# Rolling an 8192 x 8192 array: three of sixteen row groups taken through SBUF instead of copied inside HBM

## The chip, the cores and the metric

One core of one Trainium2 chip runs the program. Times are device microseconds (us) of that core; the number for a kernel is the median over its runs. "HBM" is the large memory in which the input and the output lie, "SBUF" the core's own memory of 128 partitions. "DMA" is a transfer: an instruction on one of the core's queues that 16 DMA engines of the core then carry out. Three queues issue such instructions here: SP (SyncE), ACT (ScalarE) and POOL (GpSimd). No TensorE work is done.

## The reference

```python
def setup_inputs():
    return {"x": np.random.randn(8192, 8192).astype(np.float32), "shift": 100}

def reference(x, shift):
    return np.roll(x, shift, axis=1)
```

Each row of 8192 float32 numbers (32,768 bytes) is rotated right by 100 columns: columns 100 to 8191 of the output are columns 0 to 8091 of the input, and columns 0 to 99 are the last 100 of the input. Nothing is computed; 268.44 MB are read and 268.44 MB are written.

## The kernel before

With the shift `s` = 100, `a` = 128 is the shift rounded up to a multiple of 128, and `g` = `a - s` = 28. Each output row is made in two parts: the **body**, columns 128 to 8191 (32,256 bytes), and the **head**, columns 0 to 127 (512 bytes).

**The body** is copied from HBM to HBM without passing through SBUF (L36 to L41). The rows stand in 128 blocks of 64 rows. One DMA takes the 16 rows `c*64 + e*4 + j` for e = 0 to 15, one row for each DMA engine, 504 KB in all; j runs over 0 to 3, and even j go to the SP queue, odd j to the ACT queue (L41). In the last four blocks each row is cut in two at column `mid`, so these DMAs are of 248 and 256 KB (L38). That is 528 DMAs, 264 on each queue. They depend on nothing but a free place: the framework hands eight completion semaphores round to the DMAs of SP and ACT together, and a DMA whose semaphore is still in use waits on its queue until the earlier DMA with it has landed. So at most eight of these DMAs are under way, four to a queue.

**The heads** go through SBUF on the POOL queue (L58 to L78), in 16 groups of 512 rows, four rows to a partition. For each group, POOL issues a load of 512-byte pieces that holds the tail of one row and the start of the next (`t`, L70), a load of the last row's 100 columns (L71) and a load of the first row's 28 columns (L74); VectorE (DVE) puts the pieces together in `h` (L72, L75). After the loads of all 16 groups, POOL issues 16 stores of 256 KB (L78).

Of the kernel before, what the change touches and what calls it, by code (L numbers as in the profile page):

```python
# [1 line left out]

# [4 lines left out]


@with_exitstack
def kernel(  # L10
    ctx: ExitStack,
    tc: tile.TileContext,
    x: bass.AP,
    shift: int,
    out: bass.AP,
):
    nc = tc.nc
    n_rows, n_cols = x.shape
    s = shift % n_cols
    a = -(-s // 128) * 128  # L20
    g = a - s
    P = nc.NUM_PARTITIONS
    engines = [nc.sync, nc.scalar]
    n_chunks = 16
    rows = n_rows // n_chunks

    xm = x.rearrange("(c e j) w -> c j e w", e=16, j=4)
    om = out.rearrange("(c e j) w -> c j e w", e=16, j=4)
    if a < n_cols:
        blocks = n_rows // 64
        mid = (a + n_cols) // 256 * 128  # L36
        for c in range(blocks):
            parts = ((a, mid), (mid, n_cols)) if c >= blocks - 4 and a < mid else ((a, n_cols),)  # L38
            for j in range(4):
                for lo, hi in parts:  # L40
                    engines[j % 2].dma_start(out=om[c, j, :, lo:hi], in_=xm[c, j, :, lo - s:hi - s])  # L41
    if a == 0:
        return


    if a > 512:
        for i in range(n_chunks):
            r = slice(i * rows, (i + 1) * rows)
            nc.gpsimd.dma_start(out=out[r, :s], in_=x[r, n_cols - s:])
            if g > 0:  # L50
                nc.gpsimd.dma_start(out=out[r, s:a], in_=x[r, :g])
        return

    Q = 4  # L58
    n_st = n_rows // (P * Q)
    reads = ctx.enter_context(tc.tile_pool(name="reads", bufs=n_st))  # L60
    heads = ctx.enter_context(tc.tile_pool(name="heads", bufs=n_st))
    xt = x.rearrange("(k p q) c -> k p q c", q=Q, p=P)
    ot = out.rearrange("(k p q) c -> k p q c", q=Q, p=P)
    tiles = []
    for k in range(n_st):
        t = reads.tile([P, Q - 1, a], x.dtype)
        h = heads.tile([P, Q, a], x.dtype)
        lead = bass.AP(tensor=x.tensor, offset=(k * P * Q + 1) * n_cols - s,
                       ap=[[Q * n_cols, P], [n_cols, Q - 1], [1, a]])
        nc.gpsimd.dma_start(out=t[:], in_=lead, single_packet=True)  # L70
        nc.gpsimd.dma_start(out=h[:, Q - 1, :s], in_=xt[k, :, Q - 1, n_cols - s:], single_packet=True)  # L71
        nc.vector.tensor_copy(h[:, :Q - 1, :s], t[:, :, :s])  # L72
        if g > 0:
            nc.gpsimd.dma_start(out=h[:, 0, s:], in_=xt[k, :, 0, :g], single_packet=True)  # L74
            nc.vector.tensor_copy(h[:, 1:, s:], t[:, :, s:])  # L75
        tiles.append(h)
    for k, h in enumerate(tiles):
        nc.gpsimd.dma_start(out=ot[k, :, :, :a], in_=h[:], single_packet=True)  # L78


# [1 line left out]
_INS = ['x', 'shift']  # L82
_OUTS = [((8192, 8192), 'float32')]

_NUMBERS = {'shift': 100}


# [26 lines left out]
```

## Time and profile before

| | |
|---|---|
| Median of 3 runs | 830.12 us (828.03 to 830.18) |
| Profiled execution: span from first to last instruction | 818.3 us |
| Profiled execution: time outside that span | not printed; the median lies 11.8 us above the span |
| DVE busy | 7.8 us, 32 instructions |
| POOL busy | 41.1 us, 68 instructions |
| DMAs of the body, issue to landing | 12.5 us (median, 504 KB) |
| Loads of `t` on POOL, issue to landing | 32.6 us (median, 192 KB) |
| Stores of `h` on POOL, issue to landing | 63.0 us (median, 256 KB) |
| Issuing one DMA: SP, ACT | 510 ns, 517 ns (median) |

How to read it: the line "DMA" of the page gives, in 40 equal slices, the busy share of the 16 DMA engines in tenths, and "GB/s" what they moved. The part on queues gives for each queue its packets, its bytes and the time that its packets took, as a share of the time of all 16 engines: q1 and q10 are the queues of SP and ACT (the body), q0 that of POOL (the heads). A DMA from HBM to HBM counts once in the bytes that the engines moved, and twice in the traffic of HBM, for it is read there and written there. The same answers can be had for any stretch of the span, and rates below are made from them: bytes of a stretch by its length, or bytes of a queue by the engine time that its share stands for (share times 16 engines times length).

### The profile page before, as it was taken

Reading aid. Unit: us, or ns where it says so; the run is one execution under the profiler, and the core shown is the slowest. Engines: PE = TensorE matmul, PEld = TensorE weight load, DVE = VectorE, ACT = ScalarE, POOL = GpSimd, SP = SyncE. Lnnn points to the kernel's source line nnn. Section 1 sums busy time; section 2 is a strip of 40 time slices with the busy share of each in tenths; the row PEclk is TensorE's granted clock in tenths of the full one; section 3 lists DMA queues with packets and bytes.
Section 4 is the critical chain, followed back from the end, with each engine's and each line's share of the span. In section 5 each row is a group of like instructions: output and inputs, shape, how many; then the busy total and the mean of one; then the engine's idle time right before and its main releaser. Section 6 shows DMA issues by size and latency. Waiting matters only on the chain. (4 is left out here: it accounts for less than half of the span.)

```text
span 818.3 us, 689 instructions
## 1 busy us (share of the span) xinstructions
DVE 7.8 (1%) x32; POOL 41.1 (5%) x68
## 2 busy tenths in 40 slices
DVE  0000000000000000000000000000000000000000
POOL 3011111111010000000000000000000000000000
DMA  9999999999999999999999999999999999999998
GB/s 304 340 344 338 341 334 345 341 346 350 353 352 357 347 332 321 335 328 326 333 330 323 330 331 330 331 326 333 330 328 334 333 330 339 328 333 334 328 318 294
DMA packets 20229, 272.71 MB, mean 333 GB/s; under 512 B 9472, under 2 KB 9728, under 8 KB 11776
## 3 DMA queue, kind: packets, MB, share of 16 engines
q1 hardware_dynamic: 8448, 132.14, 48.2%
q10 hardware_dynamic: 8448, 132.14, 46.1%
q0 software_dynamic: 3328, 8.39, 4.7%
q14 instruction: 5, 0.04, 0.0%
HBM read 268.44 MB, written 268.44 MB: 656 GB/s over the span
## 5 line engine op out<-in xcount | busy, mean ns | idle before, releaser
L78 POOL DMA_DIRECT2D out_dram<-h x16 | 11.4, 712 | 87.2 <-DMA out_dram<-h 51.7
L70 POOL DMA_DIRECT2D t<-in_x_dram x16 | 12.1, 759 | 32.1 <-DMA h<-in_x_dram 31.3
L74 POOL DMA_DIRECT2D h<-in_x_dram x16 | 8.6, 538 | 85.7 <-DMA t<-in_x_dram 85.7
L71 POOL DMA_DIRECT2D h<-in_x_dram x16 | 8.9, 558 | 23.9 <-DMA h<-in_x_dram 23.9
L72 DVE COPY h<-t 128x300 f32<-128x300 f32 x16 | 5.9, 368 | 190.4 <-DMA t<-in_x_dram 190.4
L75 DVE COPY h<-t 128x84 f32<-128x84 f32 x16 | 3.2, 201 | 0.0
L95 POOL MEMSET const-float32-0.0<- 128x1 f32 x1 | 0.1, 99 | 0.2 <-issue 0.2
L95 POOL MEMSET const-bfloat16-1.0<- 128x1 bf16 x1 | 0.1, 101 | 0.0
L95 POOL MEMSET const-uint8-127<- 128x1 uint8 x1 | 0.1, 99 | 0.0
L95 POOL MEMSET const-float32-1.0<- 128x1 f32 x1 | 0.1, 98 | 0.0
## 6 DMA issues: line engine op xcount, KB each, us to landing
out_dram<-in_x_dram ACTq DMA_DIRECT2D x248, 504.0 KB, 12.5
out_dram<-in_x_dram SPq DMA_DIRECT2D x248, 504.0 KB, 12.5
out_dram<-h POOLq DMA_DIRECT2D x16, 256.0 KB, 63.0
t<-in_x_dram POOLq DMA_DIRECT2D x16, 192.0 KB, 32.6
out_dram<-in_x_dram SPq DMA_DIRECT2D x8, 256.0 KB, 5.9
out_dram<-in_x_dram ACTq DMA_DIRECT2D x8, 256.0 KB, 5.8
out_dram<-in_x_dram SPq DMA_DIRECT2D x8, 248.0 KB, 6.1
out_dram<-in_x_dram ACTq DMA_DIRECT2D x8, 248.0 KB, 6.1
```

The lines of the kernel that those rows point to most:

```text
L70: nc.gpsimd.dma_start(out=t[:], in_=lead, single_packet=True)
L71: nc.gpsimd.dma_start(out=h[:, Q - 1, :s], in_=xt[k, :, Q - 1, n_cols - s:], single_packet=True)
L72: nc.vector.tensor_copy(h[:, :Q - 1, :s], t[:, :, :s])
L74: nc.gpsimd.dma_start(out=h[:, 0, s:], in_=xt[k, :, 0, :g], single_packet=True)
L75: nc.vector.tensor_copy(h[:, 1:, s:], t[:, :, s:])
L78: nc.gpsimd.dma_start(out=ot[k, :, :, :a], in_=h[:], single_packet=True)
L95: nc = _bacc.Bacc("TRN2", target_bir_lowering=False, num_devices=1)
```

## The change

The last three groups of 512 rows (rows 6656 to 8191) are taken out of the copies and of the heads. Each goes whole through one SBUF tile `stage` of 128 partitions by 4 rows by 8192 columns (128 KB in each partition, one buffer). A group is loaded by 17 DMAs: the last 100 columns of all its rows (`wrap`, pieces of 400 bytes), then 16 pieces of 128 partitions by 2048 columns (`load`, 1 MB each, rows of 8192 bytes in a partition), already shifted by 100 columns in SBUF; the last of each row has 1948 columns. It is stored by 16 DMAs of 128 by 2048 (`store`). Loads and stores are issued by SP and ACT, in one sequence with the copies, which alternates between the two queues.

The order is written out in advance: six phases, load and store of each of the three groups, each with one sixth of the copies; after each move so many copies are issued as are due. A store waits for the loads whose columns it holds, and a load of the next group for the stores that read its place. The 416 blocks-and-j of copies that remain cover rows 0 to 6655; the last two blocks, not the last four, have their rows cut at `mid`. The heads of 13 groups stay on POOL as they were (L96 to L104 of the changed file).

```diff
-    engines = [nc.sync, nc.scalar]
+    rings = [nc.sync, nc.scalar]
+    n_staged = 3
+    n_copied = n_groups - n_staged
...
-        blocks = n_rows // 64
-        for c in range(blocks):
-            parts = ((a, mid), (mid, n_cols)) if c >= blocks - 4 and a < mid else ((a, n_cols),)
-            for j in range(4):
-                for lo, hi in parts:
-                    engines[j % 2].dma_start(out=om[c, j, :, lo:hi], in_=xm[c, j, :, lo - s:hi - s])
+    def copy(c, j, lo, hi):
+        return lambda ring: ring.dma_start(out=om[c, j, :, lo:hi], in_=xm[c, j, :, lo - s:hi - s])
+    blocks = n_copied * G // 64
...
+        parts = ((a, mid), (mid, n_cols)) if c >= blocks - 2 else ((a, n_cols),)
+        for j in range(4):
+            copies += [(copy(c, j, lo, hi), hi - lo) for lo, hi in parts]
+    stage = ctx.enter_context(tc.tile_pool(name="stage", bufs=1)).tile([P, Q, n_cols], x.dtype)
+    W = 2048
+    def load(k, q, lo):
+        hi = min(lo + W, n_cols - s)
+        return lambda ring: ring.dma_start(out=stage[:, q, lo + s:hi + s], in_=xt[k, :, q, lo:hi])
+    def wrap(k):
+        return lambda ring: ring.dma_start(out=stage[:, :, :s], in_=xt[k, :, :, n_cols - s:])
+    def store(k, q, lo):
+        return lambda ring: ring.dma_start(out=ot[k, :, q, lo:lo + W], in_=stage[:, q, lo:lo + W])
+    phases = []
+    for k in range(n_copied, n_groups):
+        spots = [(q, lo) for q in range(Q) for lo in range(0, n_cols, W)]
+        phases.append([wrap(k)] + [load(k, *at) for at in spots])
+        phases.append([store(k, *at) for at in spots])
+    total = sum(w for _, w in copies)
+    issued, done, todo = 0, 0, list(copies)
+    for n, side in enumerate(phases):
+        begin, end = total * n / len(phases), total * (n + 1) / len(phases)
+        for i, move in enumerate(side):
+            move(rings[issued % 2])
+            issued += 1
+            upto = begin + (end - begin) * (i + 1) / len(side)
+            while todo and done < upto:
+                one, w = todo.pop(0)
+                one(rings[issued % 2])
+                issued += 1
+                done += w
...
-    for k in range(n_st):
+    for k in range(n_copied):
```

More of the change, by code (lines that the diff above doesn't have):

```diff
@@ L22 @@
     P = nc.NUM_PARTITIONS
-    engines = [nc.sync, nc.scalar]
-    n_chunks = 16
-    rows = n_rows // n_chunks
+    rings = [nc.sync, nc.scalar]
+    Q = 4
+    G = P * Q
+    n_groups = n_rows // G
+    if a == 0 or a > 512:
+        for i in range(n_groups):
+            r = slice(i * G, (i + 1) * G)
+            rings[i % 2].dma_start(out=out[r, s:], in_=x[r, :n_cols - s])
+            if s > 0:
+                nc.gpsimd.dma_start(out=out[r, :s], in_=x[r, n_cols - s:])
+        return
+    n_staged = 3
@@ L32 @@
+    n_copied = n_groups - n_staged
+    xt = x.rearrange("(k p q) c -> k p q c", q=Q, p=P)
+    ot = out.rearrange("(k p q) c -> k p q c", q=Q, p=P)
     xm = x.rearrange("(c e j) w -> c j e w", e=16, j=4)
     om = out.rearrange("(c e j) w -> c j e w", e=16, j=4)
-    if a < n_cols:
-        blocks = n_rows // 64
-        mid = (a + n_cols) // 256 * 128
-        for c in range(blocks):
-            parts = ((a, mid), (mid, n_cols)) if c >= blocks - 4 and a < mid else ((a, n_cols),)
-            for j in range(4):
-                for lo, hi in parts:
-                    engines[j % 2].dma_start(out=om[c, j, :, lo:hi], in_=xm[c, j, :, lo - s:hi - s])
@@ L42 @@
[L42 to L62, printed above, removed]
@@ L63 @@
-    ot = out.rearrange("(k p q) c -> k p q c", q=Q, p=P)
+    def copy(c, j, lo, hi):
+        return lambda ring: ring.dma_start(out=om[c, j, :, lo:hi], in_=xm[c, j, :, lo - s:hi - s])
+    blocks = n_copied * G // 64
+    mid = (a + n_cols) // 256 * 128
+    copies = []
+    for c in range(blocks):
+        parts = ((a, mid), (mid, n_cols)) if c >= blocks - 2 else ((a, n_cols),)
+        for j in range(4):
+            copies += [(copy(c, j, lo, hi), hi - lo) for lo, hi in parts]
+    stage = ctx.enter_context(tc.tile_pool(name="stage", bufs=1)).tile([P, Q, n_cols], x.dtype)
@@ L64 @@
+    reads = ctx.enter_context(tc.tile_pool(name="reads", bufs=n_copied))
+    heads = ctx.enter_context(tc.tile_pool(name="heads", bufs=n_copied))
     tiles = []
-    for k in range(n_st):
+    for k in range(n_copied):
         t = reads.tile([P, Q - 1, a], x.dtype)
         h = heads.tile([P, Q, a], x.dtype)
-        lead = bass.AP(tensor=x.tensor, offset=(k * P * Q + 1) * n_cols - s,
+        lead = bass.AP(tensor=x.tensor, offset=(k * G + 1) * n_cols - s,
                        ap=[[Q * n_cols, P], [n_cols, Q - 1], [1, a]])
```

## The prediction, made before the changed kernel had run

> **What bounds the kernel now.** I read the page's DMA part first, then the engines, then the queues stretch by stretch. The compute engines are idle (DVE 7.8 us, POOL 41.1 us of 818.3). From the page:
>
> ```profile
> span 818.3 us, 689 instructions
> ...
> DMA  9999999999999999999999999999999999999998
> GB/s 304 340 344 338 341 334 345 341 346 350 353 352 357 347 332 321 335 328 326 333 330 323 330 331 330 331 326 333 330 328 334 333 330 339 328 333 334 328 318 294
> DMA packets 20229, 272.71 MB, mean 333 GB/s; under 512 B 9472, under 2 KB 9728, under 8 KB 11776
> ...
> HBM read 268.44 MB, written 268.44 MB: 656 GB/s over the span
> ```
>
> The DMA engines are busy in every slice. But the GB/s line has two levels: about 345 in slices 1 to 13, while the heads pass through SBUF, and 330 after. If the engines themselves were the limit, the small pieces of the heads should have lowered the rate. So I ask for the queues in three stretches: heads being loaded (20 to 174 us), heads being stored (205 to 270) and copies alone (330 to 800).
>
> ```profile
> DMA packets 4846, 52.57 MB, mean 341 GB/s; under 512 B 2190, under 2 KB 2412, under 8 KB 3333
> ...
> q1 hardware_dynamic: 1515, 24.65, 44.0%
> q10 hardware_dynamic: 1498, 24.16, 40.1%
> q0 software_dynamic: 1833, 3.76, 15.2%
> ```
> ```profile
> DMA packets 2030, 23.15 MB, mean 356 GB/s; under 512 B 790, under 2 KB 790, under 8 KB 1386
> ...
> q1 hardware_dynamic: 644, 10.42, 47.3%
> q10 hardware_dynamic: 639, 10.26, 43.0%
> q0 software_dynamic: 744, 2.44, 10.8%
> ```
> ```profile
> DMA packets 9801, 155.07 MB, mean 330 GB/s; under 512 B 4902, under 2 KB 4902, under 8 KB 4902
> ...
> q1 hardware_dynamic: 4901, 77.44, 50.4%
> q10 hardware_dynamic: 4897, 77.62, 48.9%
> ```
>
> Two numbers come out of each. First, HBM traffic, copies (q1, q10) counted twice and heads once: loading (2 x 48.81 + 3.76) / 154 = 658 GB/s; storing (2 x 20.68 + 2.44) / 65 = 674; copies alone 2 x 155.06 / 470 = 660. Within 2% it is the same. Second, what one engine moves for a copy while it works on one (bytes by share times 16 engines times length): alone 155.06 MB / (0.993 x 16 x 470) = 20.8 GB/s; beside loads 48.81 / (0.841 x 16 x 154) = 23.6; beside stores 20.68 / (0.903 x 16 x 65) = 22.0. A copy goes faster on its engine when other engines do something that loads HBM less. Both say the same: the present bound is HBM's traffic, near 660 GB/s, and the engines are "busy" with copies that wait for it.
>
> The issuing queues are no bound. SP's waits:
>
> ```profile
> SPq L41 <- DMA out_dram<-in_x_dram: 671.1, 260, 4.8
> ```
>
> 260 of its 264 DMAs wait for a place; issuing costs 264 x 0.51 = 135 us beside 671 us of waiting.
>
> **The change part by part.**
>
> *HBM traffic: nothing.* Copies: 6656 rows x 32,256 B = 214.70 MB, counted twice 429.4; heads of 6656 rows 3.41 MB in and out, 6.8; staged rows 1536 x 32,768 B = 50.33 MB in and 50.33 out, 100.7. Sum 536.9 MB, as before (2 x 268.44). At the whole-span rate of 656 GB/s: 818 us. This is the bound if only traffic decides.
>
> *Engine work: much more.* Bytes through the engines were 272.7 MB and become 214.7 + 6.8 + 100.7 = 322.2 MB. To end in 818 us the engines must move 394 GB/s; the best stretch above had 356. The room is the time in which copies now wait. How much there is, the trace bounds by the fastest copy rate of one queue: q10 beside loads, 24.16 MB / (0.401 x 16 x 154) = 24.5 GB/s for each engine, 391 for 16. At that rate for all large transfers: (214.7 + 100.7) / 391 = 807 us, plus the heads: q0 has 4.7% of the engines' time, 38.5 us, of which 13/16, 31.2. Together 838 us, and 2 us for the three `wrap` loads, whose 400-byte pieces are like the loads of the heads (0.61 MB at 3.76 / (0.152 x 16 x 154) = 10.0 GB/s for each engine: 3.8 us of all 16, against 1.6 already counted). Divided by the 99% that the engines are busy: 848 us.
>
> *Price of a staged byte.* Not shown as such: pieces of 8 KB on the hardware queues. Nearest rows: q0's stores, 2.44 / (0.108 x 16 x 65) = 21.7 GB/s for each engine with pieces of 512 B; q0's loads at 10.0; copies with pieces of 32 KB at 24.5. With 21.7 for all staged bytes, and copies at 23.6 beside loads and 22.0 beside stores: 107.35/23.6 + 107.35/22.0 + 100.7/21.7 ms over 16 engines = 879, plus 31, 910 us. That is the upper end; 10.0 belongs to 112- to 512-byte pieces and is not taken. The larger piece is nearer to the copies' 24.5.
>
> The Trainium skill, DMA: Bandwidth & Descriptors, section Specifications, gives the 16 engines a fabric ceiling of 435 GB/s; by it the large transfers would take an estimated 725 us and the engines would never bind. No row here reaches it: the highest, of one queue, is 391 for 16 engines, so the trace neither shows nor excludes it.
>
> *The sum.* HBM alone gives 818, engines at their fastest seen 848, and the two limits now lie close. A limit in such a system is not sharp: when at some moment most engines hold loads, HBM is under-used; when most hold copies, engines wait. I take the middle, span 834, 16 us more. The median of the runs shown is 11.8 us above the span (the page prints no other time for the profiled execution); I keep this. **Forecast: 846 us.**
>
> *Waits added.* Loads and stores stand in the same SP and ACT queues as the copies, so a waiting store holds the copies behind it. But a store needs loads of its columns, some 88 DMAs earlier in the joint sequence, with eight under way and 12.5 us to landing; the changed program's order gives the stores a single semaphore, and only one `wrap` has two. I take nothing. If each of the five borders emptied the queues once: 5 x 12.5 = 62 us, 880 in all.
>
> *Issuing.* 523 DMAs on SP and ACT in place of 528, hidden by the waits above. *POOL and DVE* lose 3/16: not on the path, which is DMA throughout. *Ends.* The first 20 us ran at 304 GB/s, the last 18 at 292; cuts in two blocks instead of four, and a 1 MB store among the last DMAs: 0 to 3 us, within the range.
>
> **The rivals.**
>
> *Traffic alone decides* (engines have room to spare): span 818, time 827 to 838. For it: 658, 674 and 660 stay level while q0's share of bytes goes from 0 to 10.5%. Against: from now on it would be 31%.
>
> *Faster: uneven traffic suits HBM.* Beside stores the traffic was 674, 2% over copies alone, at 10.5% of the bytes; beside loads 658, no gain. If only these levels hold: 268.4/658 + 268.4/674 = 806, with 5 us for the slow ends 811, time 823. If the gain of the stores grows with their share, threefold, to 700: 408 + 383 + 5 = 796, time 808. It decides if the engines then move over 394 GB/s. Against: this is above all that the trace shows, and loads, half of the staging, showed none of it.
>
> *One direction is capped.* A load phase reads 16.78 + 35.78 + 0.57 = 53.1 MB and writes less; the highest read rate of a stretch is 341 GB/s and the highest write rate 356. Were these caps: 3 x 53.1/341 + 3 x 53.1/356 = 915 us, time 927. For it: nothing exceeds them. Against: they are above copies alone (330), so they rose as soon as something else let them. The Trainium skill (same page, section Where 436 GB/s comes from) lets a core's share of HBM, about 358 GB/s, bind transfers between HBM and SBUF, by which the six phases would take an estimated 890 us; the 356 here lies just under it. But its HBM Reference, section Specifications (TRN2), has a core that streams alone at about 425.
>
> *It does not do what it says* (loads and copies fall apart in time): this is the case of the borders, 880 us, 892 with the rest.
>
> **How the numbers follow.** Forecast case, two soft limits, 838 to 875: 0.46. Traffic alone, 827 to 838: 0.17, of which 0.09 within 0.3% of 830.1 (2.5 us, about what a measurement of this kernel can tell from no change), 0.06 above and 0.02 below. Faster by uneven traffic, 800 to 827: 0.25. Capped direction or emptied queues, 875 to 927: 0.12. So faster 0.27, same 0.09, slower 0.64. Range 806 to 895: it leaves out the edge of the gain and most of the caps.
>
> **What would show it.** Right: phases of about 139 us, HBM traffic 640 to 655 GB/s through the span, payload near 385, copies at 24 GB/s or more for each engine, engines busy over 97%. Traffic alone: 656 to 662 over the span. Faster: store phases above 674. Capped: load and store phases at 341 to 360 of one-way traffic, copies slower on their engine than 22. Borders: slices of the DMA line below 9 at each sixth. I am wrong in size if staged pieces of 8 KB take much more or less than 24.5 GB/s for each engine, and in sign if HBM gives above 665 GB/s to an uneven mix.

## The result, and the profile after

| | Before | After |
|---|---|---|
| Median | 830.15 us (828.03 to 831.99, 4 runs) | 854.43 us (852.77 to 856.33, 4 runs) |
| Ratio, 95% interval | | 1.0297 (1.0272 to 1.0322) |
| Profiled execution: time, span | not printed, 818.3 | 852.77, 851.0 |

The kernel became 3% slower. (Ratios here and below leave out an execution more than 1.5% above the fastest of its kernel; there was one, in e5_even16.) From the page of the changed kernel:

```profile
span 851.0 us, 664 instructions
...
GB/s 328 406 387 392 403 399 402 386 398 383 387 375 350 361 384 378 396 378 373 398 382 357 353 404 394 385 379 367 383 398 367 400 384 378 349 389 393 376 372 272
DMA packets 31685, 322.25 MB, mean 379 GB/s; under 512 B 10736, under 2 KB 10944, under 8 KB 14144
...
q10 hardware_dynamic: 13952, 158.87, 48.8%
q1 hardware_dynamic: 15024, 156.52, 47.9%
q0 software_dynamic: 2704, 6.82, 2.5%
...
HBM read 268.44 MB, written 268.44 MB: 631 GB/s over the span
```

The engines move 322.25 MB, as worked out, and they move them faster (379 GB/s in place of 333). HBM carries the same bytes as before, but only 631 GB/s of them in place of 656. The shares of the queues add up to 99.2%, so the engines were busy all the same. The GB/s line is more uneven than that of before: 349 beside 389, 353 beside 404. That unevenness is what the experiments are about.

### The profile page after: what moved, and what is told of

Same layout as the page of the kernel before. It is cut to its first block, busy times and chain, and to the rows that moved or that the text cites. A ratio compares the mean times of both kernels' runs of the same rounds, so it can differ in the third digit from the quotient of the medians.

```text
span 851.0 us, 664 instructions
## 1 busy us (share of the span) xinstructions
DVE 6.3 (1%) x26; POOL 33.4 (4%) x56
## 2 busy tenths in 40 slices
DMA packets 31685, 322.25 MB, mean 379 GB/s; under 512 B 10736, under 2 KB 10944, under 8 KB 14144
## 5 line engine op out<-in xcount | busy, mean ns | idle before, releaser
L104 POOL DMA_DIRECT2D out_dram<-h x13 | 9.2, 711 | 39.0 <-DMA out_dram<-h 25.0
L96 POOL DMA_DIRECT2D t<-in_x_dram x13 | 9.9, 762 | 16.3 <-DMA h<-in_x_dram 15.5
L100 POOL DMA_DIRECT2D h<-in_x_dram x13 | 7.0, 539 | 40.8 <-DMA t<-in_x_dram 40.8
L97 POOL DMA_DIRECT2D h<-in_x_dram x13 | 7.3, 558 | 9.6 <-DMA h<-in_x_dram 9.2
```

## The experiments

Three theories stood at the start. **A**: HBM traffic and the engines now limit by turns. At times most engines hold staged packets, which load HBM once, and the engines' own rate decides; at times nearly all hold copies, and HBM decides. What matters is how evenly the two are mixed. **B**: each staged byte costs engine time, however it is mixed. **C**: the loss is at the two ends of the span.

All ratios are against the kernel before, run beside the changed form on the same chip.

| Run | What differs from the changed kernel | Median, us | Before | Ratio, 95% interval |
|---|---|---|---|---|
| e0_before | (the kernel before) | 827.7 | 826.8 | one execution |
| e1_split_queues | staged moves on ACT, copies on SP, 16 KB pieces | 908.7 | 826.8 | 1.099 (1.098 to 1.101) |
| e2_w4096 | 16 KB pieces, 2 MB per DMA | 847.4 | 826.8 | 1.025 (1.022 to 1.028) |
| e3_one_group | one group | 836.8 | 826.8 | 1.013 (1.011 to 1.016) |
| e5_even16 | 16 partitions, 512 KB per DMA | 884.2 | 827.3 | 1.066 (1.058 to 1.073) |
| e5_even32 | 32 partitions, 512 KB per DMA | 834.6 | 827.3 | 1.009 (1.006 to 1.013) |
| e5_even16_one | 16 partitions, 512 KB, one group | 829.5 | 827.3 | 1.003 (1.001 to 1.004) |
| e6_fours | four staged moves at a time | 890.5 | 827.3 | 1.077 (1.074 to 1.079) |
| e7_even64 | 64 partitions, 512 KB per DMA | 826.6 | 818.7 | 1.009 (1.007 to 1.011) |
| e7_w1024 | 128 partitions, 4 KB pieces, 512 KB | 828.3 | 818.7 | 1.012 (1.010 to 1.014) |
| e8_even32_one | 32 partitions, 512 KB, one group | 818.1 | 818.7 | 1.000 (0.999 to 1.001) |
| e9_w8192 | whole rows, 4 MB per DMA | 866.3 | 828.1 | 1.047 (1.044 to 1.050) |

**The kernel before once more.**

> The kernel before, unchanged, profiled once more. The changed kernel's profiled execution took 852.8 us with a span of 851.0, so 1.8 us lie outside the span. If that is general, this execution's time is about 2 us above its span too, and the 818.3 us of the first profile belonged to an execution about 10 us below the median; then the span here is 818 to 830 us. If the kernel before really has 11.8 us outside its span, the span is near 818 and the time near 830.

```profile
span 826.0 us, 689 instructions
...
HBM read 268.44 MB, written 268.44 MB: 650 GB/s over the span
```

This execution took 827.74 us, 1.7 above its span. So the 11.8 us of the prediction were hardly time outside the span: the first profile most likely belonged to an execution some 10 us faster than the median beside it. Medians of the kernel before differ likewise between the four chips used here, 818.7 to 828.1, which is why ratios on one chip are compared below.

**Staged moves on one queue, copies on the other.**

```diff
-    W = 2048
+    W = 4096
...
-            move(rings[issued % 2])
-            issued += 1
+            move(nc.scalar)
...
-                one(rings[issued % 2])
-                issued += 1
+                one(nc.sync)
```

> Staged moves all on ACT in pieces of 16 KB (W = 4096), copies all on SP with 32 KB: an engine that takes one packet from each queue in turn always holds one staged packet to one copy, 1 to 2 in bytes, about the 31% that is to be moved. Theory A (loss from an uneven mix: both limits are close, and at times most engines hold staged packets, at times most hold copies): HBM traffic rises from 631 to 648 GB/s or more, time 820 to 838 us. Theory B (engine work: each byte that passes the engines twice costs engine time, however it is mixed): 850 to 860 us, HBM traffic near 631.

It took 908.7 us, which neither theory expected, and it did not make the mix that it was meant to make. SP's waits show why:

```profile
SPq L45 <- DMA out_dram<-in_x_dram: 394.6, 374, 1.9
SPq L45 <- DMA out_dram<-stage: 151.1, 13, 25.9
SPq L45 <- DMA stage<-in_x_dram: 128.7, 12, 12.7
```

Copies on SP waited 280 us, in 25 waits, for staged DMAs to land, since both still share the eight semaphores. The staged moves ran ahead nearly alone, until about 290 us, and the copies followed alone. So it does not tell A from B, but it measures each kind of traffic apart. Here are stretches of its trace with stores (145 to 185 us), with loads (205 to 225) and with copies only (300 to 880):

```profile
DMA packets 1151, 17.10 MB, mean 427 GB/s; under 512 B 164, under 2 KB 164, under 8 KB 164
...
q10 hardware_dynamic: 1037, 15.03, 88.5%
q1 hardware_dynamic: 114, 2.06, 12.0%
```
```profile
DMA packets 649, 8.48 MB, mean 424 GB/s; under 512 B 159, under 2 KB 159, under 8 KB 159
...
q10 hardware_dynamic: 585, 7.45, 87.5%
q1 hardware_dynamic: 64, 1.03, 12.0%
```
```profile
DMA packets 11771, 190.07 MB, mean 328 GB/s; under 512 B 5877, under 2 KB 5877, under 8 KB 5877
...
q1 hardware_dynamic: 11768, 190.04, 99.9%
```

With hardly anything but staged packets the engines move 424 to 427 GB/s in either direction; a staged packet has 26.5 GB/s of its engine (15.03 MB / (0.885 x 16 x 40 us)). That is the highest rate of the stretches read here, the engines' limit as far as the runs show, and HBM then carries (15.03 + 2 x 2.06) / 40 = 479 GB/s. Copies alone move 328, with HBM at 656. The same lines answer a rival, that a copy is simply slower on its engine than a staged packet. The few copies beside the staged packets have 2.06 / (0.120 x 16 x 40) = 26.8 GB/s of their engine, as much as these; copies alone have 190.04 / (0.999 x 16 x 580) = 20.5. So what slows a copy here is other copies, which load HBM as well. At the moments of either kind one of the two limits lies idle.

**Four staged moves at a time.** This is the plain test of A: the same DMAs on the same queues, only less evenly spread.

```diff
-            upto = begin + (end - begin) * (i + 1) / len(side)
+            upto = begin + (end - begin) * ((i + 1) // 4 * 4 if i + 1 < len(side) else len(side)) / len(side)
```

> The change with the same DMAs, but issued four staged moves at a time, two on each queue, and then the copies that are due for four: the same bytes and pieces, less evenly mixed. Theory A: more time with only staged packets and more with only copies, HBM traffic lower, 868 to 900 us (staging wholly apart from the copies took 908.7). Theory B: 850 to 860, no change.

890.5 us: A. The two kinds of stretch can be seen directly; the columns are the stretch, its length, DVE, POOL, clock, share of DMA and GB/s:

```profile
408.00:416.00 8.00, 0.00 (x0) 0.00 (x0) 1.00 1.01 409
424.00:440.00 16.00, 0.00 (x0) 0.00 (x0) 1.00 1.00 329
451.00:456.00 5.00, 0.00 (x0) 0.00 (x0) 1.00 1.00 421
464.00:480.00 16.00, 0.00 (x0) 0.00 (x0) 1.00 0.99 329
```

The timeline has four loads issued from 399 to 407 us and four stores from 443 to 451. After each burst the engines move 409 to 421 GB/s, nearly all of it staged (from 408 to 416 us the trace has 3.27 MB in 397 packets over 512 bytes, 8.2 KB each); in between they move 329, all of it copies (from 424 to 440 us 5.26 MB in 163 such packets, 32 KB each). If the whole kernel consisted of such stretches, it would take 100.7 MB / 415 + 214.7 MB / 329 = 243 + 653 = 896 us, the heads left out: this run is nearly that. Theory B, under which the same bytes take the same time, falls. The trace's records of single packets say where the time went. In the changed kernel the staged packets (7792 and 8192 bytes) took 252 us of all 16 engines and the copies' whole rows (32,256 bytes) 552; here it is 245 and 598. The staged bytes cost no more than in the changed kernel; the copies, crowded together, do.

**Smaller staged DMAs, spread more finely.** Loads and stores take every eighth, fourth or second partition (D = 8, 4, 2), or all with shorter pieces, so that each staged DMA has 512 KB, like a copy. Edit for 32 partitions:

```diff
-    W = 2048
+    W = 4096
+    D = 4
...
-        return lambda ring: ring.dma_start(out=stage[:, q, lo + s:hi + s], in_=xt[k, :, q, lo:hi])
+        return lambda ring: ring.dma_start(out=stage[b::D, q, lo + s:hi + s], in_=xt[k, b::D, q, lo:hi])
...
-        spots = [(q, lo) for q in range(Q) for lo in range(0, n_cols, W)]
+        spots = [(q, lo, b) for q in range(Q) for lo in range(0, n_cols, W) for b in range(D)]
```

With 32 partitions:

> As the run with 16 partitions, but 32 partitions (every fourth) with half rows of 16 KB: two packets for each engine, 512 KB for each staged DMA. Theory A: between that run and the change, 825 to 845 us. Theory B: 850 to 860. It also shows whether the reach of 16 partitions costs anything: then this one is the faster of the two.

834.6 us, inside A's range and outside B's: a ratio of 1.009 in place of 1.030, with the same bytes through the engines. From its page:

```profile
GB/s 338 395 401 393 398 407 399 417 404 374 384 384 405 368 380 392 384 399 389 390 398 395 385 396 391 386 379 372 383 396 393 387 386 395 380 395 390 389 392 320
...
HBM read 268.44 MB, written 268.44 MB: 646 GB/s over the span
```

The GB/s line is flatter again, near 390, and HBM is back at 646, beside 650 in e0_before. So 390 GB/s through the engines and HBM near its limit are possible together. Against the changed kernel the copies' whole rows took 534 us of all 16 engines in place of 552, which is most of the 20 us by which the span is shorter; the staged packets took 258. What the 7 us are that remain, no run takes apart.

With 16 partitions (D = 8, W = 8192):

> The staged bytes as in the change, but each staged DMA takes 16 partitions (every eighth) with whole rows of 32 KB: one packet for each engine, the same shape as a copy, and 192 such DMAs are spread among the copies, about one to two. So no engine ever has eight staged packets in a row in one queue, as it has with 128 partitions. Theory A (the loss is the uneven mix): HBM traffic 645 GB/s or more, time 822 to 840 us. Theory B (engine work of the staged bytes, however mixed): 850 to 860. If 16 partitions at a time are slower to reach than 128: over 860, with staged packets far above the 1.2 us that 32 KB need at the engines' best rate.

884.2 us: A's number missed, by the third reading that the expectation names. The trace shows which packets are slow. From its page (span 887.6 us, the longest of its four executions):

```profile
GB/s 302 329 376 340 354 333 359 379 392 395 385 369 378 383 344 383 380 333 346 352 364 380 393 389 388 378 361 327 368 336 348 357 348 369 371 374 384 381 389 304
```

The line is near 350 on average in the stretches with loads (numbers 2 to 7, 15 to 20 and 28 to 33) and near 380 in those with stores. A packet of a load (32,368 bytes) took 1.85 us on average, one of a store (32,768 bytes) 1.30. The size of the piece is not the reason: in e9_w8192, with packets of the same sizes over 128 partitions, they took 1.25 and 1.22. With 32 partitions a load packet of half the size took 0.67 us, or 1.35 for the same bytes; 0.5 us more for each of 1536 load packets is 48 us of all 16 engines, and the span is 56 us longer than there. So it is the loads into every eighth partition that are slow. Why is open. The Trainium skill, SBUF — State Buffer, section Door 1: The DMA port swizzle, ties a transfer's rate to how many of 16 SBUF ports its partitions reach; by its formula every eighth partition reaches 8 ports, every fourth all 16. The loads agree with that, but the stores, from the same partitions, show next to nothing of it, so the ports are not shown to be the cause.

With 64 partitions (D = 2, W = 2048) and with all 128 and 4 KB pieces (D = 1, W = 1024):

> As the even form with 32 partitions (834.6 us), but 64 partitions (every second) with pieces of 8 KB, the change's own piece: four packets of 8 KB for each engine, 512 KB for each staged DMA, twice as many staged DMAs as the change. Theory A (length of the run of staged packets that one DMA puts into an engine's queue decides): four against eight of the same size, 836 to 848 us, between 834.6 and 854.4. If the size of the piece decides, 850 to 856.

> All 128 partitions with pieces of 4 KB: eight packets for each engine as in the change, but half the bytes, 512 KB for each staged DMA. If the bytes of a run decide: near the other 512 KB forms, 834 to 842 us. If the number of packets in a run decides, as when engines take one packet from each queue in turn: with eight copies between eight small packets the mix is poorer still, 848 to 865.

1.009 and 1.012. (In us these expectations assumed a kernel before at 827; here it took 818.7. As ratios to 827 the 836 to 848 and 834 to 842 expected of 512 KB are 1.011 to 1.025 and 1.008 to 1.018: the first result lies just under its range, the second inside.) Neither the size of a packet nor the number of packets in a run decides: four packets of 8 KB are as good as two of 16, and eight of 4 KB nearly so. What the three forms share, and the change does not, is 512 KB for each staged DMA, and with it twice as many staged DMAs, spread more finely.

**Larger staged DMAs.** W = 4096 and W = 8192 on all partitions:

> Only W = 4096, so staged pieces of 16 KB, the queues alternating as in the change. Theory A: the mix stays uneven, 848 to 862 us. Theory B: engine work per byte stays, 850 to 856 us; if 8 KB pieces cost engines extra, 840 to 848. Mainly the control for the run with split queues: what that gains beyond this one is the queues, not the piece.

> The change with W = 8192: 128 partitions with whole rows of 32 KB, 4 MB for each staged DMA, 12 loads and 12 stores in all. So far, against the kernel before of the same call: 512 KB for each staged DMA 1.009 to 1.012, 1 MB (the change) 1.030, 2 MB 1.025. If the bytes that one staged DMA lays into an engine's queue decide, this is clearly slower than the change, ratio 1.035 or more. If the size of a packet beside the copies' 32 KB decides (the mix while one queue holds staged packets and the other copies), the mix is one to one, richer than the one to two that is needed, and the ratio is 1.02 to 1.035, about that of 2 MB.

2 MB: 847.4 us, just below the ranges of both theories and inside the 840 to 848 given for pieces of 8 KB that cost the engines extra. But the kernel before was 3 us faster here than beside the change; the ratio, 1.025, lies where both theories have it (848 us to 830 is 1.022, 856 is 1.031), so the run is no help between them. That 8 KB pieces cost no extra, the run with 64 partitions shows. 4 MB: 1.047, clearly worse, as A has it if bytes in a burst decide. From its page:

```profile
GB/s 312 409 383 360 417 386 367 407 354 390 363 430 348 329 327 407 406 359 389 392 390 355 377 359 364 379 355 320 406 410 361 380 401 379 335 401 405 324 405 285
...
HBM read 268.44 MB, written 268.44 MB: 622 GB/s over the span
```

It swings from 320 to 430. So the order is 1.009 to 1.012 with 512 KB on 32 partitions or more, 1.030 with 1 MB, 1.025 with 2 MB, 1.047 with 4 MB. The engine time of the copies' whole rows has the same order: 526 to 534 us, 552, 553 and 575. That 2 MB is no worse than 1 MB stays unexplained; the intervals of the ratios (1.022 to 1.028, 1.027 to 1.032) just touch.

**One group.** In the form of the change, then in the finer forms:

> One staged group instead of three, two phases, each with half of the copies; staged bytes are about 12% of a phase instead of 31%. Theory A: engines have room, HBM decides: 822 to 832 us, the kernel before within 0.5%; if the 674 GB/s seen beside stores holds, up to 1% faster. Theory B (cost in proportion to staged bytes, 24 us for three): 836 to 840 us. Theory C (most of the loss is at the two ends of the span, whatever is staged): 840 to 850.

> The even form with 16 partitions, one staged group instead of three (836.8 us with one group in the form of the change). Theory A: no loss left, 822 to 830 us against some 827 before; if an even mix lets HBM move more than 660 GB/s, below 820. Theory B: 835 to 838.

> The even form with 32 partitions, one staged group: the best version that the runs point to. Theory A: the loss of 7 us with three groups falls to a third, 826 to 831 us against 827 before; traffic through HBM is the same as before, so nothing below 824 is expected. Faster than before by 0.3% or more only if an even mix lets HBM move more than 660 GB/s.

The first missed A's range and lies in B's: 836.8 us, 10 us for one group where three cost 24. I had taken 12% of staged bytes to be few enough to leave HBM the only limit. A's reading, that a burst of a 1 MB DMA is as uneven when it is rare and the cost goes with the number of bursts, is argued; this run alone could not tell it from B. The same group split into 512 KB can: it costs 0.3% (16 partitions) or nothing (32 partitions, 1.000, interval 0.999 to 1.001), where B has it cost as much as before. The form with 32 partitions is the best version that the runs point to, and it does not beat the kernel before: the traffic through HBM is the same.

**Theory C.** The changed kernel in four stretches, and e0_before in three:

```profile
0.00:20.00 20.00, 0.97 (x4) 7.56 (x16) 1.00 0.90 325
20.00:140.00 120.00, 5.33 (x22) 25.87 (x41) 1.00 1.01 396
140.00:830.00 690.00, 0.00 (x0) 0.00 (x0) 1.00 1.00 381
830.00:851.00 21.00, 0.00 (x0) 0.00 (x0) 1.00 0.73 265
```
```profile
0.00:20.00 20.00, 0.48 (x2) 6.83 (x15) 1.00 0.92 301
20.00:806.00 786.00, 7.27 (x30) 34.38 (x54) 1.00 1.00 332
806.00:826.00 20.00, 0.00 (x0) 0.00 (x0) 1.00 0.88 287
```

Time lost at an end is its length times the shortfall from the middle: after, 20 x (1 - 325/381) = 2.9 and 21 x (1 - 265/381) = 6.4 us; before, 1.9 and 2.7. So the ends are 5 of the 24 us. The DMA line of the last stretch shows engines idle for about 2 us near 836, shortly before SP issues the last store at 838.4:

```profile
DMA  9688989799310009399899576998999999410000
```

Theory C is true of these few us and no more; no run moved the last store away.

## Why the prediction came out as it did, point by point

- **What bounds the kernel before: HBM traffic.** Right. Copies alone load HBM with 656 GB/s also when one queue issues them all, a copy beside staged packets is as fast on its engine as these (both e1_split_queues), and one finely mixed group changes nothing (e8_even32_one). The three levels of traffic that I read, 658, 660 and 674 GB/s, differ by 2.4%, not by less than 2.
- **HBM traffic unchanged, engine work 322.2 MB.** Right to the digit. The engine work in itself cost little: the same 322 MB go through in 1.009 of the time of before when finely mixed.
- **The engines' limit, 848 us.** Wrong. I took 24.5 GB/s for each engine from the copies of one queue, an average that has waiting for HBM in it; the trace of before has single copy packets of 1.19 us, 27.0 GB/s. Where hardly anything but staged packets was under way, 26.5 was seen, so the large transfers need 315.4 / 424 = 744 us, with my 33 for the small ones 777 (these were too high as well: q0 took 21 us after, not 31). On average the engines' limit lay below HBM's 818, not above it. The 435 GB/s of the Trainium skill's DMA: Bandwidth & Descriptors, section Specifications, was nearer to the 424 to 427 measured here than my bound of 391.
- **The sum, the middle of two limits, 834 (+16 us).** The reason given with it was right: the limit is not sharp, because at some moments most engines hold staged packets and at others copies. The term was mis-sized. 24 us were measured, of which some 5 are the ends, for which I took 0 to 3. That the 16 came as near as they did is luck: with the engines' limit at 777 the larger of the two limits is HBM's 818, and the same sum has no loss to put in the middle. What the loss follows in the runs, the bytes of one staged DMA and how finely they are spread, stood in the diff (1 MB) and I gave it no price.
- **11.8 us outside the span.** Wrong: 1.8. The 818 belonged to a fast execution. With some 828, the span that goes with the median, the middle to 848 would have been 838, and the forecast loss 10 us instead of 16, so the misplaced base moved it towards the 24 measured. The median was predicted 8 us too low, +1.9% where +3.0% came.
- **Price of a staged byte.** Near the 24.5 that I chose, far from the 21.7: a packet of 8192 bytes took 328 ns on average in the changed kernel, 25.0 GB/s for its engine, and 26.5 is what staged packets have in e1_split_queues.
- **Waits at the borders: nothing.** Right as far as seen: L63 and L66 start new phases at 145.9 and 560.7 us, so phases of about 140 (139 were forecast), and no slice of the DMA line falls below 9 before the last.
- **The signs named beforehand.** HBM 631 GB/s (640 to 655), payload 379 (near 385) and copies at 23.8 GB/s for each engine (32,256 bytes in 1.35 us; 24 or more) all came out a little low, as goes with a loss larger than forecast; the engines were busy 99.2% (over 97%).
- **Faster by uneven traffic.** Fell: no version was faster, and the finely mixed ones on 32 partitions or more bring HBM to 646 to 658 GB/s, about what the kernel before has on the same chips (some 650 and 657).
- **One direction capped.** Fell: in e1_split_queues 427 GB/s were written to HBM in one stretch and 424 read from it in another, above the 356 and 341 taken for caps. The Trainium skill's rule (DMA: Bandwidth & Descriptors, section Where 436 GB/s comes from), that HBM binds such transfers near 358, does not hold for this core, which ran alone; the figure of the Trainium skill's HBM Reference, section Specifications (TRN2), about 425 for a core that streams alone, does.
- **That it falls apart in time.** Not in the change, but e1_split_queues did so, at a ratio of 1.099.

## What to carry to other kernels

Where two kinds of transfer have different limits, as copies and staged moves have here, running them together gains only while both are in the engines at once. Look at the GB/s line and at the HBM rate of the whole span, and if the line swings between two levels, try smaller DMAs of the rarer kind, spread more finely; here 512 KB were enough, and nothing smaller was run. And ask first whether the bytes through the bounding resource get fewer: here each byte was read from HBM once and written once either way, so at the same HBM rate a perfect mix could only have drawn even.

## What the runs showed of the hardware that was not expected

A single queue with DMAs of 504 KB copies from HBM to HBM as fast as two (328 GB/s between 300 and 880 us of e1_split_queues, 328 between 330 and 800 us of e0_before). Engines that were 99% busy were not the limit: a copy held its engine for 1.57 us among copies alone and for 1.19 us among staged packets (both e1_split_queues). Loads into every eighth partition took 1.85 us for a packet of 32 KB, stores from the same partitions 1.30 (e5_even16). And the same kernel before had medians from 818.7 to 830.2 us, 818.7 on one chip and 826.8 to 828.1 on three others, so a difference of 1% between profiles of different chips says nothing.
